# One norm in three FFN stages: a sum over partitions with ones as weights, and the inverse root by ACT's root, DVE's reciprocal and a Newton step

## The chip, the core and the metric

The kernel runs on one core of one Trainium2 chip. The core has a matrix engine (PE, with its weight loads shown apart as PEld), three engines for elementwise work (DVE, ACT and POOL) and a queue that starts DMA transfers (SP). The metric is the device time of one execution in microseconds; the time of the kernel before is the median of three runs. A profiled execution has a time of its own, and a span from its first to its last instruction, which is a little shorter.

## The reference

A decoder trunk of two layers over 256 tokens with 1024 features, all in float32. Each layer is a feed-forward block (FFN), a mixer, and a second FFN, so there are four FFNs. What matters here is how an FFN begins:

```
def _rmsnorm(x, g):
    y = x * rsqrt(mean(x * x, axis=-1) + 1e-6)
    return y * g

h = h + 0.5 * ((silu(n @ w_gate) * (n @ w_up)) @ w_down),   n = _rmsnorm(h, g)
```

`w_gate` and `w_up` are 1024 x 2816, `w_down` is 2816 x 1024. The norm needs, for each token, the sum of the squares of its 1024 features, and one over the root of their mean.

## The kernel before, in words

The residual `hT` lies with features on the 128 partitions (8 tiles of 128) and the 256 tokens along the free dimension. A float32 product is made of two rounded parts, so that two PE passes give nearly full precision: `whi` and `wlo` are the high and low part of a weight chunk, and the activations stand as low and high part side by side. One pair of matmuls in `mm2` is L216 (low weights, 256 columns) and L217 (high weights, 512 columns: low and high part of the activations).

An FFN's `gate_up` goes through 11 blocks `b`. Each block takes four PSUM banks (from pools `acc` and `rot` by turns, four banks each), goes over 8 feature tiles in four steps `c` of one weight chunk each, and makes 8 x 4 = 32 pairs. `evacuate` then adds the two halves of each bank (ACT copy L324, DVE add L326), and `epilogue` multiplies by the norm factor and gates: L381, L382 (silu), L383, L384, L386, L387. Then 22 x 8 = 176 pairs of the down projection follow. The FFN is thus 352 + 176 pairs.

The weights flow by `next_chunk`: a DMA on SP brings a chunk, ACT casts it (`whi`, L169), DVE subtracts (`wlo`, L177). At each step the chunk that PE will use three steps later gets its `wlo`, and the casts run one further ahead. ACT and DVE work strictly in the order in which the program issues their instructions, so whatever stands ahead of a cast or subtraction delays it.

The norm is deferred: matmuls use the activations before scaling, and the factor per token, `rb` (with half of it, `rbh`), is applied in `epilogue`. During the end of the stage before, POOL adds the squares into one 128 x 256 tile (`norm_sq`, L278). What follows is placed by `hooks`, functions called at step `c` of block `b`. For FFN 2 to 4:

```
hooks = {1: {0: lambda: norm_sum(s, sets[0]()), 2: mid}}
```

- Block 1, step 0, `norm_sum`: two fp32 matmuls (L284, 128 x 1 each) sum over partitions, with the tokens going to the partitions; they write a bank of the pool that block 0 used, so they wait until DVE has read that bank. DVE adds epsilon (L287), POOL takes the power -1/2 (L250), splits it (L292, L293) and makes two diagonal matrices of it (L297, four instructions).
- Block 1, step 2, `mid`: `norm_row` spreads the factor over all partitions by four 128 x 128 matmuls with ones as weights (L304, L306). ACT copies the result to `rb` (L309), DVE writes `rbh` (L313), and block 0's epilogue follows (`late(0)`).

FFN 1 (other hooks) and the odd mixer use the same `norm_sum` and `norm_row` at other places.

Of the kernel before, what the change touches and what calls it, by code (L numbers as in the profile page):

```python
# [9 lines left out]
F32 = mybir.dt.float32  # L10
F32R = mybir.dt.float32r
I32 = mybir.dt.int32
AF = mybir.ActivationFunctionType
ALU = mybir.AluOpType
AX = mybir.AxisListType

P = 128
T = 256
TB = T // P
D = 1024  # L20
# [17 lines left out]
EPS = 1e-6  # L38
# [37 lines left out]
def trunk_kernel(  # L76
# [21 lines left out]
    nc = tc.nc  # L98
    PSUM = bass.MemoryType.PSUM

    const = ctx.enter_context(tc.tile_pool(name="const", bufs=1))
# [8 lines left out]
    def nm(s):  # L110
        uid[0] += 1
        return f"{s}_{uid[0]}"
# [7 lines left out]
    def small(shape, tag, bufs=2):  # L120
        return spool.tile(shape, F32, tag=tag, name=nm(tag), bufs=bufs)
# [114 lines left out]
    ones_r = const.tile([P, P], F32R, name="ones_r")  # L236
    nc.gpsimd.tensor_copy(ones_r, ones)
    cmean = const.tile([P, 3], F32, name="cmean")
    for i, n in enumerate((D, QL, KVL)):
        nc.gpsimd.memset(cmean[:, i : i + 1], 1.0 / n)  # L240
    mhalf = const.tile([P, 16], F32, name="mhalf")
    nc.gpsimd.memset(mhalf, -0.5)
    warm = const.tile([P, 2], F32, name="warm")
# [2 lines left out]
    def preload(func):  # L246
        nc.scalar.activation(warm[:, 0:1], ones[:, 0:1], func)
# [23 lines left out]
    def norm_sq(s, k, eng=nc.gpsimd):  # L271
        sq = small([P, T], "sq", bufs=3)
        nc.scalar.activation(sq, hT[:, k, :], AF.Square)
        if s.sum is None:
            s.sum = sq
        else:
            t = small([P, T], "sqsum", bufs=3)
            eng.tensor_add(t, s.sum, sq)  # L278
            s.sum = t

    def norm_sum(s, bank):
        s.bank = bank
# [71 lines left out]
    def ffn(s, nxt_args, sets, first=False):  # L354
        with tc.tile_pool(name=nm("ffn"), bufs=2) as fp:
# [47 lines left out]
            if first:  # L403
                hooks = {0: {1: lambda: nc.sync.dma_start(cst_sb, cst), 2: lambda: squares(range(4)),
                             3: lambda: squares(range(4, KD))},
                         1: {2: lambda: norm_sum(s, sets[0]())}, 2: {1: mid, 3: lambda: late(1)}}
            else:
                hooks = {1: {0: lambda: norm_sum(s, sets[0]()), 2: mid}}
            for b in range(NB):
                held[b] = evacuate(gate_up(b, hooks.get(b, {})))  # L410
                if b > (1 if first else 0):
# [649 lines left out]

    const.tile([P, 88], F32, name="align")
    spool.tile([P, 8], F32, tag="align", name="align_small", bufs=1)
    wu = const.tile([P, T], mybir.dt.bfloat16, name="wu")
    nc.vector.memset(wu, 0.0)
# [7 lines left out]
    s = norm_begin("ffn", 0)  # L1075
# [12 lines left out]
    parts = [emit_split() for _ in range(HEAD)]  # L1088
    seen = set()
    for k, c, cs in head:  # L1090
        if k not in seen:
            if k == 0:
                nc.vector.tensor_scalar(s.xh[:, k, :], hT[:, k, :], pcol(s.gname, s.goff), None,
                                        op0=ALU.mult)
# [5 lines left out]
    s = ffn(s, ("mix", 0), (acc_bank, rot_bank), first=True)  # L1100
# [85 lines left out]
```

## Time and profile before

| | |
|---|---|
| three runs | 896.54, 899.02, 899.45 us; median 899.02 |
| profiled execution, its own time | 896.36 us |
| its span | 894.6 us |
| granted TensorE clock | 0.999 |
| DMA | 164.45 MB, mean 184 GB/s |
| start of FFN 2, 3 and 4 on PE | 266.07, 450.43 and 706.34 us |

The starts of FFN 3 and 4 are those of their first pair. In a row of the timeline the columns are start in us, duration in us, engine, line, operation, output <- inputs, form, count and, in brackets, the idle time before it with what ended it. A row of groups has busy time in us and mean duration in ns behind the first bar. A matmul's duration includes its way through the array, so rows of PE overlap; what one costs is read from the distance between starts.

### The profile page before, as it was taken

How to read it: one execution, taken by the hardware profiler on the slowest of the kernel's cores; microseconds unless marked ns; L12 is line 12 of the kernel's file. 1: busy time of each engine (PE TensorE's matmuls, PEld its weight loads, DVE VectorE, ACT ScalarE, POOL GpSimd, SP SyncE). 2: the span in 40 equal slices, each digit the busy share in tenths (PEclk: the TensorE clock that was granted, in tenths of full speed). 3: DMA queues.
4: the chain of work that ended last, by engine and by line, in shares of the span. 5: the costliest groups of instructions: out<-in, count | busy, mean ns of one | idle time of the engine just before them, and what ended most of it. 6: DMA issues, size and time to landing. Idle time of an engine off the chain costs nothing.

```text
span 894.6 us, 13668 instructions
## 1 busy us (share of the span) xinstructions
PE 886.8 (99%) x5206; PEld 783.3 (88%) x5206; DVE 650.0 (73%) x997; ACT 497.8 (56%) x789; POOL 91.5 (10%) x123
## 2 busy tenths in 40 slices
PE   9999999999999999999999999999999999999998
PEld 7888888899898888888888888888888888888887
DVE  6887778658877877775558777756658878777652
ACT  7565554457675555554446555534545666555430
POOL 0200000118433000000130000001120220000000
PEclk9999999999999999999999999999999999999999
DMA  8675556644344655556644555576535456555750
GB/s 321 191 246 189 188 189 231 187 140 136 106 139 144 219 191 187 192 191 223 209 142 147 190 191 189 194 264 190 170 122 163 172 176 212 187 190 191 256 165 24
DMA packets 60257, 164.45 MB, mean 184 GB/s; under 512 B 5408, under 2 KB 7712, under 8 KB 60192
## 3 DMA queue, kind: packets, MB, share of 16 engines
q1 hardware_dynamic: 59904, 163.28, 54.6%
q8 instruction: 41, 0.67, 0.3%
q10 hardware_dynamic: 288, 0.30, 0.1%
q14 instruction: 24, 0.20, 0.1%
HBM read 162.51 MB, written 1.05 MB: 183 GB/s over the span
## 4 chain that ended last, share of the span: by engine, by line
PE 90%; DVE 5%; POOL 1%; issue 1%; ACT 1%; DMA 1%; SPq 0%; DVEq 0%; ACTq 0%; POOLq 0%
PE acc L217 27%; PE rot L217 27%; PE acc L216 14%; PE rot L216 14%; DVE wlo L177 2%; PE rot L210 1%; PE rot L212 1%; PE rot L211 1%; PE acc L211 1%; PE acc L210 1%; PE acc L212 1%; DMA raw<-w_gu 1%; POOL diag L297 0%; DVE sA L623 0%; DVE z L1006 0%
## 5 line engine op out<-in xcount | busy, mean ns | idle before, releaser
L177 DVE TENSOR_TENSOR wlo<-raw,whi 128x1024 fp32r<-128x1024 f32 (+2 forms) x298 | 352.6, 1226 | 72.0 <-ACT whi L169 72.0
L169 ACT CAST whi<-raw 128x1024 fp32r<-128x1024 f32 (+2 forms) x303 | 301.6, 1044 | 99.6 <-PE acc L217 41.3
L217 PE MATMUL acc<-x,whi 128*128 128x512 f32 x768 | 267.8, 391 | 0.0
L217 PE MATMUL rot<-x,whi 128*128 128x512 f32 x704 | 245.6, 392 | 0.0
L216 PE MATMUL acc<-x,wlo 128*128 128x256 f32 x768 | 216.2, 281 | 0.6 <-DVE wlo L182 0.5
L216 PE MATMUL rot<-x,wlo 128*128 128x256 f32 x704 | 197.5, 281 | 0.3 <-DVE wlo L177 0.3
L217 PEld LDWEIGHTS acc<-x,whi 128*128 128x128 f32 x768 | 143.8, 187 | 31.1
L217 PEld LDWEIGHTS rot<-x,whi 128*128 128x128 f32 x704 | 131.7, 187 | 29.0
L216 PEld LDWEIGHTS acc<-x,wlo 128*128 128x128 f32 x768 | 145.2, 189 | 1.5 <-DVE wlo L182 1.1
L216 PEld LDWEIGHTS rot<-x,wlo 128*128 128x128 f32 x704 | 133.1, 189 | 0.6 <-DVE wlo L177 0.6
L217 PE MATMUL rot<-pp,whi 128*128 128x512 f32 x352 | 122.2, 391 | 0.0
L217 PE MATMUL acc<-pp,whi 128*128 128x512 f32 x352 | 122.2, 391 | 0.0
L216 PE MATMUL rot<-pp,wlo 128*128 128x256 f32 x352 | 98.6, 280 | 0.0
L216 PE MATMUL acc<-pp,wlo 128*128 128x256 f32 x352 | 98.6, 280 | 0.0
L217 PEld LDWEIGHTS rot<-pp,whi 128*128 128x128 f32 x352 | 65.8, 187 | 14.4
L217 PEld LDWEIGHTS acc<-pp,whi 128*128 128x128 f32 x352 | 65.8, 187 | 14.4
L216 PEld LDWEIGHTS rot<-pp,wlo 128*128 128x128 f32 x352 | 66.5, 189 | 0.0
L216 PEld LDWEIGHTS acc<-pp,wlo 128*128 128x128 f32 x352 | 66.5, 189 | 0.0
L324 ACT COPY a<-rot 128x256 f32<-128x256 f32 x88 | 29.9, 374 | 50.5 <-PE rot L217 50.5
L382 ACT ACTIVATE gu<-gu 128x512 f32<-128x512 f32 x44 | 27.8, 632 | 52.1 <-DVE gu L381 52.1
L324 ACT COPY a<-acc 128x256 f32<-128x256 f32 x88 | 29.1, 375 | 49.3 <-PE acc L217 49.3
L326 DVE TENSOR_TENSOR gu<-acc,a 128x256 f32<-128x256 f32 x88 | 31.2, 417 | 29.5 <-ACT a L324 29.5
(250 smaller groups left out, 903.6 us busy)
## 6 DMA issues: line engine op xcount, KB each, us to landing
raw<-w_gu SPq DMA_DIRECT2D x172, 512.0 KB, 4.8
raw<-w_down SPq DMA_DIRECT2D x88, 512.0 KB, 4.7
raw<-ew_out SPq DMA_DIRECT2D x8, 512.0 KB, 3.6
raw<-ow_v SPq DMA_DIRECT2D x8, 512.0 KB, 3.5
raw<-ow_u SPq DMA_DIRECT2D x8, 512.0 KB, 4.9
raw<-ow_out SPq DMA_DIRECT2D x8, 512.0 KB, 3.8
raw<-ew_p SPq DMA_DIRECT2D x4, 512.0 KB, 3.8
raw<-w_gu SPq DMA_DIRECT2D x7, 256.0 KB, 5.3
```

Source lines behind the costliest of these rows:

```text
L169: nc.scalar.copy(hi[:, :n], r[:, :n])
L177: eng.tensor_sub(lo[:, :n], r[:, :n], hi[:, :n].bitcast(F32))
L210: nc.tensor.matmul(out, wl, xh, start=start, stop=False, skip_group_check=True)
L211: nc.tensor.matmul(out, wh, xl, start=False, stop=False, skip_group_check=True)
L212: nc.tensor.matmul(out, wh, xh, start=False, stop=stop, skip_group_check=True)
L216: nc.tensor.matmul(bank[:, 0:T], wl, x[:, 1, :], start=start, stop=False, skip_group_check=True)
L217: nc.tensor.matmul(bank, wh, x.rearrange("p s t -> p (s t)"), start=False, stop=stop, skip_group_check=True)
L324: nc.scalar.copy(tmp[:, i, :], bank[:, 0:T])
L326: nc.vector.tensor_add(out[:, i, :], bank[:, T:], tmp[:, i, :])
L382: nc.scalar.activation(t, t, AF.Silu)
```

## The change

FFN 2 to 4 compute the factor in another way; FFN 1 and the mixers keep theirs.

- `norm_parts`, block 0, step 0: POOL rounds the sum of squares to a high part and subtracts for the low part (two instructions of 128 x 256).
- `norm_all`, block 1, step 0: four 128 x 128 matmuls with ones as weights (L293 of the changed file) sum over partitions and leave the sum in every partition. ACT takes the root of 128 x 256 (with a table load ahead of it) and loads the table of silu again (`preload`). DVE writes the mean plus epsilon.
- `norm_inverse`, block 1, step 1: DVE takes the reciprocal of the root, makes one Newton step (three instructions) and halves the result into `rbh`.
- Block 1, step 2 keeps `late(0)` alone. `norm_sum` and `norm_row` go from these three FFNs.
- A column with epsilon joins the constants, and a filler tile shrinks by as much as that column takes.

```diff
+    eps_col = const.tile([P, 1], F32, name="eps_col")
+    nc.gpsimd.memset(eps_col, EPS)
...
+    def norm_parts(s, fp):
+        s.parts = fp.tile([P, 2, T], F32R, tag="parts", name=nm("parts"), bufs=1)
+        nc.gpsimd.tensor_copy(s.parts[:, 1, :], s.sum)
+        nc.gpsimd.tensor_sub(s.parts[:, 0, :], s.sum, s.parts[:, 1, :].bitcast(F32))
+
+    def norm_all(s, bank, fp):
+
+        for tb in range(TB):
+            ts = slice(tb * P, (tb + 1) * P)
+            for i in range(2):
+                nc.tensor.matmul(bank[:, ts], ones_r, s.parts[:, i, ts], start=tb == 0 and i == 0,
+                                 stop=i == 1, skip_group_check=True)
+        s.root = fp.tile([P, T], F32, tag="root", name=nm("root"), bufs=1)
+        nc.scalar.activation(s.root, bank[:, 0:T], AF.Sqrt, scale=1.0 / D, bias=eps_col)
+        preload(AF.Silu)
+        s.mean = fp.tile([P, T], F32, tag="mean", name=nm("mean"), bufs=1)
+        nc.vector.tensor_scalar(s.mean, bank[:, 0:T], 1.0 / D, EPS, op0=ALU.mult, op1=ALU.add)
+
+    def norm_inverse(s, fp):
+
+        y, t = [fp.tile([P, T], F32, tag=n, name=nm(n), bufs=1) for n in ("inv", "newton")]
+        nc.vector.reciprocal(y, s.root)
+        nc.vector.tensor_mul(t, y, y)
+        nc.vector.scalar_tensor_tensor(t, t, -0.5, s.mean, op0=ALU.mult, op1=ALU.mult)
+        s.rb = small([P, T], "rb", bufs=2)
+        nc.vector.scalar_tensor_tensor(s.rb, t, 1.5, y, op0=ALU.add, op1=ALU.mult)
+        s.rbh = small([P, T], "rbh", bufs=2)
+        nc.vector.tensor_scalar(s.rbh, s.rb, 0.5, None, op0=ALU.mult)
...
-                hooks = {1: {0: lambda: norm_sum(s, sets[0]()), 2: mid}}
+                hooks = {0: {0: lambda: norm_parts(s, fp)},
+                         1: {0: lambda: norm_all(s, sets[0](), fp), 1: lambda: norm_inverse(s, fp),
+                             2: lambda: late(0)}}
...
-    const.tile([P, 88], F32, name="align")
+    const.tile([P, 80], F32, name="align")
```

Where the instructions stand is shown at three places in FFN 2. On PE, at the turn from block 0 (bank pool `rot`) to block 1 (`acc`), before:

```order
L216 MATMUL rot_3056<-x_2455,wlo_2936 128x256
L217 MATMUL rot_3056<-x_2455,whi_2935 128x512
L284 MATMUL rot_3159<-cmean,sqsum_3046 128x1 [waits DVE_49,Pool_49]
L284 MATMUL rot_3159<-cmean,sqsum_3046 128x1
L216 MATMUL acc_3155<-x_2455,wlo_3058 128x256
L217 MATMUL acc_3155<-x_2455,whi_3057 128x512
```

At the same place, in the changed kernel:

```order
L216 MATMUL rot_3058<-x_2457,wlo_2938 128x256
L217 MATMUL rot_3058<-x_2457,whi_2937 128x512
L293 MATMUL rot_3164<-parts_3059,ones_r 128x128 [waits DVE_49,Pool_49]
L293 MATMUL rot_3164<-parts_3059,ones_r 128x128 x3
L216 MATMUL acc_3160<-x_2457,wlo_3063 128x256
L217 MATMUL acc_3160<-x_2457,whi_3062 128x512
```

The two fp32 matmuls have given way to four of 128 x 128, with waits on the same two engines; the four matmuls L304 and L306, which stood 16 pairs later, have no successor.

On ACT, from block 0's last copy to the epilogue of block 0, before:

```order
L324 COPY a_3146<-rot_3056 128x256 [waits PE_49]
L169 CAST whi_3175<-raw_3061 128x1024 [waits DMAHW4_49]
L169 CAST whi_3197<-raw_3083 128x1024 [waits DMAHW5_49,DVE_49]
L309 COPY rb_3223<-rot_3159 128x256 [waits DVE_49,PE_49]
L382 ACTIVATE gu_3145<-gu_3145 128x512 [waits DVE_49]
L386 CAST pp_3052<-gu_3145 128x2x256 [waits DVE_49]
```

The same stretch of ACT in the changed kernel:

```order
L355 COPY a_3151<-rot_3058 128x256 [waits PE_49]
L296 ACT_TABLE_LOAD
L296 ACTIVATE root_3169<-rot_3164,eps_col 128x256 [waits PE_49]
L249 ACT_TABLE_LOAD
L249 ACTIVATE warm<-ones 128x1
L169 CAST whi_3174<-raw_3066 128x1024 [waits DMAHW4_49]
L169 CAST whi_3205<-raw_3088 128x1024 [waits DMAHW5_49,DVE_49]
L413 ACTIVATE gu_3150<-gu_3150 128x512 [waits DVE_49]
L417 CAST pp_3054<-gu_3150 128x2x256 [waits DVE_49]
```

The two casts now stand behind the root and two table loads, and the copy `rb` behind them is gone.

On DVE, from block 0's last addition to the epilogue of block 0, before:

```order
L326 TENSOR_TENSOR gu_3145<-rot_3056,a_3146 128x256 [waits Activation_49]
L287 TENSOR_SCALAR me_3162<-rot_3159 128x2 [waits PE_49]
L177 TENSOR_TENSOR wlo_3124<-raw_2939,whi_3123 128x1024 [waits DMAHW3_49]
L177 TENSOR_TENSOR wlo_3176<-raw_3061,whi_3175 128x1024 [waits DMAHW4_49,Activation_49]
L313 TENSOR_SCALAR rbh_3225<-rot_3159 128x256 [waits Activation_49]
L381 TENSOR_TENSOR gu_3145<-gu_3145,rb_3223 128x512 [waits DVE_49]
```

The same stretch of DVE in the changed kernel:

```order
L357 TENSOR_TENSOR gu_3150<-rot_3058,a_3151 128x256 [waits Activation_49]
L299 TENSOR_SCALAR mean_3172<-rot_3164 128x256 [waits Activation_49]
L177 TENSOR_TENSOR wlo_3129<-raw_2941,whi_3128 128x1024 [waits DMAHW3_49]
L304 RECIPROCAL inv_3196<-root_3169 128x256
L305 TENSOR_TENSOR newton_3197<-inv_3196 128x256 [waits DVE_49]
L306 SCALAR_TENSOR_TENSOR newton_3197<-newton_3197,mean_3172 128x256 [waits DVE_49]
L308 SCALAR_TENSOR_TENSOR rb_3201<-newton_3197,inv_3196 128x256 [waits DVE_49]
L310 TENSOR_SCALAR rbh_3203<-rb_3201 128x256 [waits DVE_49]
L177 TENSOR_TENSOR wlo_3175<-raw_3066,whi_3174 128x1024 [waits DMAHW4_49,Activation_49]
L412 TENSOR_TENSOR gu_3150<-gu_3150,rb_3201 128x512
```

The first instruction behind the additions now waits for ACT, and five instructions stand ahead of the second `wlo`.

## The prediction

> **What bounds the kernel now.** The profile's page comes first: its span, its busy times, and the chain that ended last by engine.
>
> ```profile
> span 894.6 us, 13668 instructions
> PE 886.8 (99%) x5206; PEld 783.3 (88%) x5206; DVE 650.0 (73%) x997; ACT 497.8 (56%) x789; POOL 91.5 (10%) x123
> PE 90%; DVE 5%; POOL 1%; issue 1%; ACT 1%; DMA 1%; SPq 0%; DVEq 0%; ACTq 0%; POOLq 0%
> ```
>
> PE holds 90% of the chain. So the change is worth the PE time that it frees, less any time that it makes PE wait. PE's timeline next, around the two places in FFN 2 where the norm sits (L284 and L304 to L306).
>
> ```profile
> 277.03 0.28 PE L216 MATMUL rot<-x,wlo 128*128 128x256 f32 x1
> 277.50 0.58 PE L284 MATMUL rot<-cmean,sqsum 128*128 128x1 f32 x4
> 278.38 0.28 PE L216 MATMUL acc<-x,wlo 128*128 128x256 f32 x1
> ...
> 283.23 0.28 PE L216 MATMUL acc<-x,wlo 128*128 128x256 f32 x1
> 283.58 0.22 PE L304 MATMUL rot<-diag,ones_r 128*128 128x128 f32 x1
> 284.37 0.28 PE L216 MATMUL acc<-x,wlo 128*128 128x256 f32 x1
> ```
>
> From 278.38 to 283.23 there are 14 pairs, 0.346 us each. In both disturbed stretches two pairs are made as well, so what exceeds 2 x 0.35 is the norm's: 1.35 - 0.70 = 0.65 us for L284, and 1.14 - 0.69 = 0.45 us for the four L304 and L306. The same rows in FFN 3, FFN 4 and, for L284 alone, FFN 1:
>
> ```profile
> 461.18 0.28 PE L216 MATMUL acc<-x,wlo 128*128 128x256 f32 x1
> 461.66 0.58 PE L284 MATMUL acc<-cmean,sqsum 128*128 128x1 f32 x4
> 462.54 0.28 PE L216 MATMUL rot<-x,wlo 128*128 128x256 f32 x1
> 467.39 0.28 PE L216 MATMUL rot<-x,wlo 128*128 128x256 f32 x1
> 468.53 0.28 PE L216 MATMUL rot<-x,wlo 128*128 128x256 f32 x1
> 717.30 0.28 PE L216 MATMUL rot<-x,wlo 128*128 128x256 f32 x1
> 717.77 0.58 PE L284 MATMUL rot<-cmean,sqsum 128*128 128x1 f32 x4
> 718.65 0.28 PE L216 MATMUL acc<-x,wlo 128*128 128x256 f32 x1
> 723.50 0.28 PE L216 MATMUL acc<-x,wlo 128*128 128x256 f32 x1
> 724.64 0.28 PE L216 MATMUL acc<-x,wlo 128*128 128x256 f32 x1
> ...
> 22.73 0.28 PE L216 MATMUL rot<-x,wlo 128*128 128x256 f32 x1
> 23.08 0.50 PE L284 MATMUL acc<-cmean,sqsum 128*128 128x1 f32 x4
> 23.88 0.28 PE L216 MATMUL rot<-x,wlo 128*128 128x256 f32 x1
> ```
>
> FFN 3 gives 1.36 - 0.69 = 0.67 and 1.14 - 0.69 = 0.45 us, FFN 4 1.35 - 0.70 = 0.65 and 0.45 us. All the norm's PE time that the change touches is therefore 1.97 + 1.35 = 3.32 us of the span; no more than that can be freed on PE. In FFN 1 L284 follows one pair (0.35) after 22.73 and costs 1.15 - 0.69 = 0.46 us; in FFN 2 to 4 it starts some 0.13 us after its turn and costs 0.2 more. The reason stands in DVE's timeline in FFN 2 (the fourth row is PE's):
>
> ```profile
> 276.93 1.48 DVE L326 TENSOR_TENSOR gu<-rot,a 128x256 f32<-128x256 f32 x4 [1.95 <-ACT a L324]
> 284.57 0.43 DVE L313 TENSOR_SCALAR rbh<-rot 128x256 f32<-128x256 f32 x1 [3.83 <-ACT rb L309]
> 295.27 4.63 DVE L177 TENSOR_TENSOR wlo<-raw,whi 128x1024 fp32r<-128x1024 f32 x4
> ...
> 297.90 0.28 PE L216 MATMUL rot<-x,wlo 128*128 128x256 f32 x1
> ```
>
> The first of four additions ends near 276.93 + 0.42 = 277.35 us, past the slot for L284 at 277.03 + 0.35 = 277.38 once the signal has travelled; the norm's bank is the one that it reads.
>
> **PE's part of the change.** The fp32 sums and the spreading go, -3.32 us. Four 128 x 128 matmuls with ones as weights come, in the first place's position. They are of the form of L304 and L306, so 0.45 us each time. They write the same pool's bank, so they wait for the same addition: between 0 and 0.2 us more (FFN 1 against FFN 2 to 4). I take the 0.13 by which L284 starts late, since weights that are ones can be loaded during it. That makes 0.58 us three times, 1.74 us, with ends of 1.35 and 1.95. **PE gains 3.32 - 1.74 = 1.6 us, between 1.4 and 2.0.**
>
> **POOL.** Its first instructions must end before block 1. The sum of squares ends here:
>
> ```profile
> 265.62 6.01 POOL L278 TENSOR_TENSOR sqsum<-sqsum,sq 128x256 f32<-128x256 f32 x6
> ```
>
> At 271.63, that is; two more of that size take about 2 us (6.01 / 6 each) and end near 273.6, 3.9 us ahead of the matmuls. The power, the split and the diagonals that POOL loses were waited for by nothing that bounds: PE took up L304 one pair after 283.23. Cost nothing.
>
> **ACT.** Its timeline, in FFN 2 and, for a table load, in FFN 4:
>
> ```profile
> 277.85 2.00 ACT L169 CAST whi<-raw 128x1024 fp32r<-128x1024 f32 x2
> 284.17 0.37 ACT L309 COPY rb<-rot 128x256 f32<-128x256 f32 x1 [4.32 <-PE rot L306]
> 724.83 1.28 ACT L382 ACT_TABLE_LOAD   x1
> 726.13 0.63 ACT L382 ACTIVATE gu<-gu 128x512 f32<-128x512 f32 x1
> ```
>
> After the copies, at 277.85, come a load (to 279.1), the root (0.37 for the copy's size, at most 0.63, the activation of twice the size: to 279.6), the second load (to 280.9), a small activation (0.2, my estimate, below the copy's 0.37) and the two casts, 281.1 to 283.1, which now end 3.3 us later than at 279.85. The 4.32 us in which ACT waited for the spread sum take that up. Six loads come, and the one in FFN 4 goes.
>
> **DVE.** The rows that price its instructions are groups:
>
> ```profile
> L177 DVE TENSOR_TENSOR wlo<-raw,whi 128x1024 fp32r<-128x1024 f32 x292 | 346.3, 1230 | 66.3 <-ACT whi L169 66.3
> L872 DVE RECIPROCAL rs<-sums 128x2 f32<-128x2 f32 x8 | 1.2, 153 | 0.0
> L287 DVE TENSOR_SCALAR me<-acc 128x2 f32<-128x2 f32 x4 | 0.6, 156 | 7.9 <-PE acc L284 7.9
> L1006 DVE SCALAR_TENSOR_TENSOR z<-rot,par_h,row_sb 128x256 f32<-128x256 f32 x6 | 2.6, 478 | 0.0
> ```
>
> `mean` waits for the root, as `rbh` waited for `rb` (both read one bank), so DVE idles from 278.4 to 279.65, and the `wlo` behind it waits too. Then `mean` (0.43, to 280.1), `wlo` (to 281.3), the reciprocal, the product (0.43), two steps of 0.48, the halving (0.43), and the second `wlo`. No row shows a reciprocal of 256 columns. At two columns it takes 153 ns against 156 for a plain instruction, so 0.43 us is the near end, and I take it; from the far side, `wlo` has at most 1.2 ns per column and pass (1230 / 1024), and I carry the case of several passes as a rival. By the near end the chain ends at 283.5 and the second `wlo` at 284.7, and block 0's epilogue starts at 284.7, where it started near 284.9 before.
>
> PE needs the first of these chunks at block 1's fourth step, about 286, and the second at block 2's first, about 289; both are met. The tightest place is later: the first `wlo` of the group at 295.27 ends by 296.5, and PE needs it at block 2's fourth step, 297.90, so 1.4 us are left. After the change PE comes 0.5 us earlier and DVE 0.2, so about **1.1 us of cover are left. The ACT and DVE chain costs nothing, and each us beyond this cover costs one in each of three FFNs.** FFN 3 and 4 have the same order of work.
>
> A rule speaks against this edit: the Trainium skill, in "ScalarE: Activation LUTs", What ACT_TABLE_LOAD costs, counts 1.28 us for a load and 1.38 for a drain at every switch, and advises batching by table set. The trace agrees with the load, 1.28 us, and shows no drain, for the next activation starts 1.30 after it. By the page's sum the chain would be 1.4 us longer on DVE, and the forecast 3 x 0.3 = 0.9 us less of a gain.
>
> **The sum.** 896.36 - 1.6 = 894.8 us for an execution like the profiled one. That one lies 2.66 us under the median of 899.02 (its own time is 1.8 above its span), so against the median: **897.4 us**, 0.18% less. About 0.3%, 2.7 us, is what a measurement of this kernel can tell from no change, so this counts as the same.
>
> **The rivals.** *PE keeps a slower beat* (slower). Its pairs have two paces. In the table by stretch, FFN 2's block 0 before L284 (the columns are length, busy time and count of L217 alone on PE and PEld, clock, DMA):
>
> ```profile
> 266.07:277.03 10.96, 10.84 (x31) 5.83 (x31) 1.00 0.43 139
> ...
> 692.22 0.50 PE L217 MATMUL rot<-zz,whi 128*128 128x512 f32 x1 [0.20 <-DVE zz L1016]
> ```
>
> 31 pairs in 10.96 us are 0.3535 each, at a granted clock of 1.00; after L284 it is 0.346. The second row is a wait after which the same slow pace set in and held until FFN 4's L284. If the new matmuls don't end it as L284 did, the 528 - 32 = 496 later pairs of an FFN cost 496 x 0.007 = 3.5 us. Since a slow FFN 2 hands its pace on to FFN 3, and FFN 4 meets the same, all three is the likelier form: 897.4 + 10.5 = 907.9; FFN 4 alone gives 900.9. Against it: after each group of four short matmuls L304 and L306 the pairs ran at 0.346 to 0.35. But those came out of the quick pace, and the new ones meet the slow one in FFN 2 and 4, with a wait. It makes the kernel slower by over 0.3% from two FFNs on (897.4 + 7.0 = 904.4).
>
> *The reciprocal passes many times over its data.* At eight passes, 8 x 256 x 1.2 ns = 2.5 us, 2.1 more than taken; PE waits 2.1 - 1.1 = 1.0 us in each FFN, 3.0 in all, 897.4 + 3.0 = 900.4, still within 0.3%. For it speaks only that no row is long enough; against it the 153 ns. The Trainium skill, "VectorE: DVE Perf Modes", First, the fixed hardware budget, has the reciprocal as an iterated division with a repeat count of 8. The trace has two columns only, too few to show this.
>
> *The matmuls save nothing*, if bank wait and weights cost what the second place gave up: 899.0. Against it, PE loses a whole place.
>
> *More than 0.3% faster* would take 0.9 of the 1.1 us in each FFN, which four matmuls of 0.45 leave no room for. Only a displacement of the whole measurement, whose runs spread over 2.9 us, could show it.
>
> **How the numbers follow.** Forecast 0.60, the slower beat in two or three FFNs 0.12 and in one 0.03, many passes 0.08, no saving 0.07, faster by more 0.10. Same is 0.60 + 0.03 + 0.08 + 0.07 = 0.78, slower 0.12, faster 0.10. The range goes from the lowest run less the gain, 896.54 - 1.6 = 894.9, to the slower beat in one FFN, 900.9; it takes in the many passes and no saving, and leaves out the slower beat in more FFNs.
>
> **What would show it.** Right: PE's rows have one disturbed stretch per FFN with 1.2 to 1.35 us for two pairs, 0.346 per pair behind it, no PE row with a wait on DVE's `wlo` L177 in blocks 1 and 2, table loads of 1.28 us, and a reciprocal of about 0.43. Wrong: pairs at 0.3535 after block 0, a wait at block 2's fourth step, or the first new matmul more than 0.2 us after its turn.

## The result, and the profile after

The changed kernel takes 902.52 us (median of 9 runs, 899.28 to 905.65); the kernel before, run beside it, 898.74 (9 runs, 895.72 to 900.28). The ratio is 1.0058, with an interval of 1.0041 to 1.0075: slower by 0.6%, where a gain of 0.18% was forecast. The profiled execution took 902.24 us, its span 5.6 us more than the one before. The nine runs lie in three groups some 3 us apart (one at 899.3, four at 902.1 to 902.5, four at 905.1 to 905.7), about what one FFN costs more at the slower of the prediction's two paces, 3.5 us. So the number of FFNs at that pace seems to differ from run to run; in both profiled executions FFN 1 goes at the quicker one. First the changed kernel's page (span, busy times, chain by engine), to be held against the three rows that open the prediction.

```profile
span 900.2 us, 13647 instructions
PE 892.0 (99%) x5194; PEld 782.5 (87%) x5194; DVE 661.7 (74%) x1009; ACT 505.5 (56%) x797; POOL 86.1 (10%) x109
PE 88%; DVE 7%; issue 2%; ACT 1%; POOL 1%; DMA 1%; SPq 0%; DVEq 0%; ACTq 0%; POOLq 0%
```

PE has 12 matmuls fewer and is busy 5.2 us longer. Where that lies is shown by counts in equal stretches. In the table by stretch, for L217 alone as in the prediction, these are 100 us each of FFN 1, FFN 2, FFN 3 and FFN 4:

```profile
80.00:180.00 100.00, 100.00 (x290) 53.94 (x289) 1.00 0.60 202
330.00:430.00 100.00, 100.00 (x285) 53.19 (x284) 1.00 0.60 203
520.00:620.00 100.00, 100.00 (x284) 53.18 (x284) 1.00 0.60 201
770.00:870.00 100.00, 100.00 (x289) 53.87 (x289) 1.00 0.60 200
```

The kernel before has 289 or 290 in all four; its rows of FFN 2 and 3:

```profile
330.00:430.00 100.00, 100.00 (x289) 53.88 (x289) 1.00 0.62 207
520.00:620.00 100.00, 100.00 (x290) 53.89 (x289) 1.00 0.61 199
```

In FFN 2 and 3 the changed kernel makes 4 to 6 fewer at the same granted clock of 1.00: it goes at the slower of the two paces that the prediction described. From the starts to the nanosecond these are 346.7 and 353.3 ns per pair; 6.67 ns apart, 3.5 us for an FFN's 528 pairs.

PE's timeline shows where it starts in FFN 2. The first three rows are at the norm (L293), the last three at block 2's fourth step.

```profile
277.24 0.28 PE L216 MATMUL rot<-x,wlo 128*128 128x256 f32 x1
277.71 0.63 PE L293 MATMUL rot<-parts,ones_r 128*128 128x128 f32 x4
278.59 0.28 PE L216 MATMUL acc<-x,wlo 128*128 128x256 f32 x1
...
297.32 0.28 PE L216 MATMUL rot<-x,wlo 128*128 128x256 f32 x1
297.66 0.32 PE L216 MATMUL rot<-x,wlo 128*128 128x256 f32 x1
298.04 0.28 PE L216 MATMUL rot<-x,wlo 128*128 128x256 f32 x1
```

FFN 2 begins slow in both kernels, and behind the norm the pairs take 346.7 ns here too. The pair begun at 297.66 takes 0.38 us, 0.035 too long, and from there on every pair takes 353.3 ns: the last 440 of FFN 2 and all of FFN 3. What came late is `wlo`; DVE's timeline tells why:

```profile
277.14 1.48 DVE L357 TENSOR_TENSOR gu<-rot,a 128x256 f32<-128x256 f32 x4 [1.18 <-ACT a L355]
279.99 0.43 DVE L299 TENSOR_SCALAR mean<-rot 128x256 f32<-128x256 f32 x1 [1.36 <-ACT root L296]
281.46 1.75 DVE L304 RECIPROCAL inv<-root 128x256 f32<-128x256 f32 x1
...
285.96 0.68 DVE L412 TENSOR_TENSOR gu<-gu,rb 128x512 f32<-128x512 f32 x1
...
296.32 3.49 DVE L177 TENSOR_TENSOR wlo<-raw,whi 128x1024 fp32r<-128x1024 f32 x3
```

The reciprocal takes 1.75 us. Block 0's epilogue starts at 285.96 instead of some 284.9, and the `wlo` group behind it at 296.32 instead of 295.27: 1.05 us later, while PE is there 0.24 us earlier. Of the cover of 1.4 us that the prediction measured, 1.29 is spent on this, and the 0.1 left is less than the weight load ahead of the matmul takes (189 ns, the mean of L216's loads). ACT went as foretold:

```profile
278.18 1.28 ACT L296 ACT_TABLE_LOAD   x1
279.48 0.47 ACT L296 ACTIVATE root<-rot,eps_col 128x256 f32<-128x256 f32 x1
279.97 1.28 ACT L249 ACT_TABLE_LOAD   x1
```

In FFN 3 the norm meets the slow pace, and the pace goes on behind it. In FFN 4 the norm waits; the rows are of PE, of DVE and of POOL:

```profile
464.11 0.28 PE L216 MATMUL acc<-x,wlo 128*128 128x256 f32 x1
464.65 0.63 PE L293 MATMUL acc<-parts,ones_r 128*128 128x128 f32 x4
465.53 0.28 PE L216 MATMUL rot<-x,wlo 128*128 128x256 f32 x1
...
722.54 0.27 PE L216 MATMUL rot<-x,wlo 128*128 128x256 f32 x1
723.86 0.63 PE L293 MATMUL rot<-parts,ones_r 128*128 128x128 f32 x4 [0.81 <-DVE gu L357]
724.74 0.28 PE L216 MATMUL acc<-x,wlo 128*128 128x256 f32 x1
...
717.71 5.68 DVE L177 TENSOR_TENSOR wlo<-raw,whi 128x1024 fp32r<-128x1024 f32 x4 [0.99 <-ACT whi L169]
723.31 1.40 DVE L357 TENSOR_TENSOR gu<-rot,a 128x256 f32<-128x256 f32 x4
...
718.21 1.27 POOL L285 CAST parts<-sqsum 128x256 fp32r<-128x256 f32 x1
719.56 1.60 POOL L286 TENSOR_TENSOR parts<-sqsum,parts 128x256 fp32r<-128x256 f32 x1
```

The same place in the kernel before, on DVE:

```profile
712.08 4.92 DVE L177 TENSOR_TENSOR wlo<-raw,whi 128x1024 fp32r<-128x1024 f32 x4 [0.98 <-ACT whi L169]
```

With POOL's two new instructions beside them the four `wlo` take 5.68 us, not 4.92. The additions that free the norm's bank start only at 723.31, 0.4 after PE's turn, and PE waits 0.81 us.

The time adds up by stage, from start to start on PE. FFN 2 goes from 184.36 to 186.86 us: 440 x 6.67 ns = 2.93 for the pace, 0.04 for the wait, less 0.45 that the norm got shorter (0.65 + 0.45 before, 1.35 - 0.70 = 0.65 after), makes 2.52; measured 2.50. FFN 3 with the stage behind it, up to the wait near that stage's end (the prediction's row at 692.22 us): 528 x 6.67 ns = 3.52, less 0.40 (1.12 to 1.42 - 0.70 = 0.72), makes 3.12; measured 3.08. FFN 4's norm costs 2.20 - 0.70 = 1.50 instead of 1.10, and its first 30 pairs are quick where they were slow; measured 0.17 more. The rest is -0.1: FFN 2 starts 0.22 later, and from that wait to FFN 4 it is 0.34 less, in the main since the pairs there are slow before and quick now.

### The profile page after: what moved, and what is told of

The parts are those of the page before. It is cut to its first block, busy times and chain, and to the rows that moved or that the text cites. A ratio compares the mean times of both kernels' runs of the same rounds, so it can differ in the third digit from the quotient of the medians.

```text
span 900.2 us, 13647 instructions
## 1 busy us (share of the span) xinstructions
PE 892.0 (99%) x5194; PEld 782.5 (87%) x5194; DVE 661.7 (74%) x1009; ACT 505.5 (56%) x797; POOL 86.1 (10%) x109
## 3 DMA queue, kind: packets, MB, share of 16 engines
HBM read 162.51 MB, written 1.05 MB: 182 GB/s over the span
## 4 chain that ended last, share of the span: by engine, by line
PE 88%; DVE 7%; issue 2%; ACT 1%; POOL 1%; DMA 1%; SPq 0%; DVEq 0%; ACTq 0%; POOLq 0%
PE acc L217 26%; PE rot L217 26%; PE acc L216 14%; PE rot L216 13%; DVE wlo L177 2%; PE rot L210 1%; PE rot L212 1%; PE rot L211 1%; DVE par_h L361 1%; PE acc L211 1%; PE acc L210 1%; PE acc L212 1%; DMA raw<-w_gu 1%; ACT whi L169 1%; POOL diag L328 0%
## 5 line engine op out<-in xcount | busy, mean ns | idle before, releaser
L217 PE MATMUL acc<-x,whi 128*128 128x512 f32 x768 | 270.1, 395 | 0.0
L217 PE MATMUL rot<-x,whi 128*128 128x512 f32 x704 | 247.3, 395 | 0.0
L216 PE MATMUL acc<-x,wlo 128*128 128x256 f32 x768 | 216.5, 282 | 0.2
L216 PE MATMUL rot<-x,wlo 128*128 128x256 f32 x704 | 197.6, 281 | 0.3 <-DVE wlo L177 0.3
L217 PEld LDWEIGHTS acc<-x,whi 128*128 128x128 f32 x768 | 144.2, 188 | 33.1
L217 PEld LDWEIGHTS rot<-x,whi 128*128 128x128 f32 x704 | 132.0, 187 | 30.7
L216 PEld LDWEIGHTS acc<-x,wlo 128*128 128x128 f32 x768 | 145.3, 189 | 1.6 <-DVE wlo L182 1.2
L216 PEld LDWEIGHTS rot<-x,wlo 128*128 128x128 f32 x704 | 133.0, 189 | 0.7 <-DVE wlo L177 0.6
L217 PE MATMUL rot<-pp,whi 128*128 128x512 f32 x352 | 123.4, 395 | 0.0
L217 PE MATMUL acc<-pp,whi 128*128 128x512 f32 x352 | 123.4, 395 | 0.0
L216 PE MATMUL acc<-pp,wlo 128*128 128x256 f32 x352 | 98.7, 280 | 0.0
L216 PE MATMUL rot<-pp,wlo 128*128 128x256 f32 x352 | 98.7, 280 | 0.0
L217 PEld LDWEIGHTS rot<-pp,whi 128*128 128x128 f32 x352 | 66.0, 187 | 15.5
L217 PEld LDWEIGHTS acc<-pp,whi 128*128 128x128 f32 x352 | 66.0, 187 | 15.5
L216 PEld LDWEIGHTS rot<-pp,wlo 128*128 128x128 f32 x352 | 66.5, 189 | 0.0
L216 PEld LDWEIGHTS acc<-pp,wlo 128*128 128x128 f32 x352 | 66.5, 189 | 0.0
L357 DVE TENSOR_TENSOR gu<-rot,a 128x256 f32<-128x256 f32 x88 | 31.4, 418 | 29.3 <-ACT a L355 29.3
```

The source lines that it names most:

```text
L216: nc.tensor.matmul(bank[:, 0:T], wl, x[:, 1, :], start=start, stop=False, skip_group_check=True)
L217: nc.tensor.matmul(bank, wh, x.rearrange("p s t -> p (s t)"), start=False, stop=stop, skip_group_check=True)
L357: nc.vector.tensor_add(out[:, i, :], bank[:, T:], tmp[:, i, :])
```

## The experiments

The letters of the theories are those of the text on record ahead of each run, and a letter of one group of runs need not mean the same in the next. Ratios are against runs of the kernel before on the same chip. "Slow" and "quick" mean the pace, 353.3 and 346.7 ns a pair.

**What starts the slow pace?** The kernel before, with a reciprocal that nothing reads behind `late(0)`:

```diff
+            def extra():
+                y = fp.tile([P, T], F32, tag="extra", name=nm("extra"), bufs=1)
+                nc.vector.reciprocal(y, s.rb)
...
-                hooks = {1: {0: lambda: norm_sum(s, sets[0]()), 2: mid}}
+                hooks = {1: {0: lambda: norm_sum(s, sets[0]()), 2: lambda: (mid(), extra())}}
```

> The kernel before with one more DVE instruction, a reciprocal of 128 x 256 into a tile that nobody reads, behind block 0's epilogue in FFN 2 to 4. It takes 1.75 us, the cover at block 2's fourth step was 1.4 us, so the wlo there comes about 0.3 us late. Norm, matmuls, POOL and tables are as before. Theory A: PE waits 0.3 us there in each FFN (0.9), and the beat behind it is 0.3533 in some of the three FFNs until the next norm's fp32 sums end it, 3.1 us for each FFN: 897.3 with none, 900.4 with one, 906.6 with three. Theory B: the beat stays 0.3467 behind that wait, 897.3.

902.26 us, ratio 1.0053 (1.0034 to 1.0072). PE's timeline in FFN 2, block 2's fourth step, and the table by stretch:

```profile
297.54 0.28 PE L216 MATMUL rot<-x,wlo 128*128 128x256 f32 x1
298.12 0.39 PE L216 MATMUL rot<-x,wlo 128*128 128x256 f32 x1
298.58 0.28 PE L216 MATMUL rot<-x,wlo 128*128 128x256 f32 x1
```

```profile
330.00:430.00 100.00, 100.00 (x284) 53.18 (x283) 1.00 0.60 201
520.00:620.00 100.00, 100.00 (x284) 53.18 (x283) 1.00 0.59 200
770.00:870.00 100.00, 100.00 (x290) 53.99 (x289) 1.00 0.59 201
```

Two pairs take 0.58 and 0.46 us, 0.35 over their time; behind them FFN 2 is slow, FFN 3 likewise, FFN 4 waits and stays quick. A late `wlo` alone starts the slow pace, though not every time: in FFN 1, where all kernels wait for a `wlo` at some 49 us, 7 of 20 profiles are slow behind it. The same with two plain products (0.43 us each) in the reciprocal's place:

> As the run with the reciprocal, but with two products of 128 x 256 instead, 0.85 us, which lies within the cover of 1.4 us. Theory A: no wait at block 2's fourth step, 0.3467 behind it, time as before, 896.4 in an execution like the profiled one. A delay that counts whether or not it is covered would give 3 x 0.85 = 2.6 us more, 899.

896.93 us, ratio 0.9996 (0.9984 to 1.0008). As long as DVE stays inside its cover, its extra work costs nothing.

**Is the late `wlo` all?** The changed kernel with `mean` moved from `norm_all` into `norm_inverse`, ahead of the reciprocal and behind the first `wlo`, so that DVE idles 0.23 us for the root and not 1.36:

```diff
-        nc.vector.tensor_scalar(s.mean, bank[:, 0:T], 1.0 / D, EPS, op0=ALU.mult, op1=ALU.add)
+        s.bank = bank
...
+        nc.vector.tensor_scalar(s.mean, s.bank[:, 0:T], 1.0 / D, EPS, op0=ALU.mult, op1=ALU.add)
```

> The changed kernel with one DVE instruction moved: mean stands behind the first wlo of block 1 instead of ahead of it, so that DVE works on that wlo while it would wait for the root; the chain behind ends about 1.2 us earlier. Theory A (late weights set the beat): the wlo for block 2's fourth step, which came 0.04 us late in FFN 2 of the changed kernel, is in time; FFN 2 keeps 0.3467 us per pair behind its norm, FFN 3 takes that over, and the two stages lose the 6.2 us of the slow beat: 896 to 897 us. Theory B (the four matmuls at the norm set the beat, whatever DVE does): 0.3533 in FFN 3 as before, and in FFN 2 from the norm or later: 899 to 902. Theory C (the loss is the sum of waits, the beat is nothing to do with it): 0.1 us less than the changed kernel, 902.

905.74 us, ratio 1.0095 (1.0072 to 1.0119). No `wlo` is late in FFN 2 to 4, and yet FFN 2 and 3 are slow from end to end. The rows of both:

```profile
330.00:430.00 100.00, 100.00 (x284) 53.18 (x284) 1.00 0.58 195
520.00:620.00 100.00, 100.00 (x284) 53.18 (x283) 1.00 0.59 201
```

FFN 2 begins slow, as it does in every profile; behind the norm it is still slow, and FFN 3 is handed the same. So the new matmuls don't end the slow pace every time. Over all profiles with them the pairs went quick behind 7 of the 12 that met it; behind the old sums in the same place of FFN 2 to 4, which waited too, in 7 of 8. These are too few to tell the two apart, but the old kernel had `norm_row` behind them and the new one has nothing. The changed kernel with the old sums (two fp32 matmuls, 128 x 1) put back at block 3, as a reset:

```diff
+            def reset(bank):
+                for tb in range(TB):
+                    nc.tensor.matmul(bank[:, tb : tb + 1], s.sum[:, tb * P : (tb + 1) * P],
+                                     cmean[:, 0:1], start=True, stop=True)
...
+                         3: {0: lambda: reset(sets[0]())}}
```

> The changed kernel with two fp32 matmuls of the old norm (128 x 1, result unused) at block 3's first step in FFN 2 to 4. They cost PE about 0.65 us each time, 2.0 in all. Theories A and B: they end a slow beat as they did in the kernel before; behind block 3 all three FFNs run at 0.3467, so FFN 2 and FFN 3 win back about 2.9 us each of 3.1 and 3.5: 902.2 - 5.8 + 2.0 = 898.4. Theory C: only the cost shows, 904.2. If the slow beat goes on behind them, what ended it in the kernel before was not these matmuls.

905.77 us, ratio 1.0085 (1.0065 to 1.0104). Neither expected time came out. The sums wait for their bank; behind them FFN 2 stays slow, FFN 3 goes from slow to quick, FFN 4 from quick to slow. A group that waits is no sure reset.

**POOL beside DVE.** The changed kernel with one fp32 product of 128 x 256 on the sum itself, without POOL's parts:

```diff
-                nc.tensor.matmul(bank[:, ts], ones_r, s.parts[:, i, ts], start=tb == 0 and i == 0,
-                                 stop=i == 1, skip_group_check=True)
+        nc.tensor.matmul(bank[:, 0:T], ones, s.sum, start=True, stop=True)
...
-                hooks = {0: {0: lambda: norm_parts(s, fp)},
```

> The changed kernel with the sum over partitions as one fp32 128x256 product on the sum of squares itself, in place of GpSimd's two parts and the four 128x128 products. Theory C (FFN4's wait of 0.81 us ahead of the norm comes from the parts on GpSimd running beside VectorE's wlo and slowing both): without the parts the four wlo of FFN4 take 4.9 us as before the change, not 5.7, the additions come earlier, and the wait falls to 0.1 to 0.3; the fp32 product itself takes 0.4 to 0.7 us in place of four times 0.11. With the beat left to chance the time is 899 to 903. Rival (the wait is from the bank's own late addition whatever GpSimd does): the wait in FFN4 stays at 0.6 to 0.9.

904.95 us, ratio 1.0087 (1.0071 to 1.0104). FFN 4 on PE and DVE:

```profile
723.47 0.28 PE L216 MATMUL rot<-x,wlo 128*128 128x256 f32 x1
723.94 0.67 PE L290 MATMUL rot<-sqsum,ones 128*128 128x256 f32 x2
724.80 0.28 PE L216 MATMUL acc<-x,wlo 128*128 128x256 f32 x1
...
718.29 4.93 DVE L177 TENSOR_TENSOR wlo<-raw,whi 128x1024 fp32r<-128x1024 f32 x4 [0.97 <-ACT whi L169]
```

Theory C holds: `wlo` takes 4.93 us again, and the norm costs 1.33 - 0.70 = 0.63, not 1.50. The time rises all the same: FFN 2 and 3 are slow and FFN 4 is from its block 2's fourth step on, where a `wlo` is late. With the stretch ahead of FFN 4 that makes 1559 slow pairs in the profile against 995 of the changed kernel.

**A group that waits for nothing.** In the kernel before, `norm_row`'s four matmuls (L304, L306) had nothing to wait for. e1 with four such products in their old place (`four`: ones by `parts`, into the other half of the norm's bank; nothing reads them):

```diff
-                              2: lambda: late(0)}}
+                              2: lambda: (four(s.bank, s.parts), late(0))}}
```

> The kernel of e1_mean_behind_wlo with, in FFN 2 to 4, four more 128x128 products (ones by the parts of the sums, into the other half of the norm's bank) in block 1 ahead of its third step, where norm_row's four stood before; nothing reads them and they wait for nothing that is still under way. Theory A (the time lost in the changed kernel is TensorE's slower beat, and what used to end it was norm_row's short group that waits for nothing): from that place FFN 2, 3 and 4 show pairs of 346 to 347 ns whatever they had ahead of it, unless a late wlo comes behind it; the four cost 3 x 0.45 us, and the time falls from 905.7 of e1 to 898 to 900, with FFN1's own beat as before. Rival (the group ends nothing; chance or the wait decides): slow pairs go on behind block 1's third step in two of the three FFNs and the time stays at 902 to 907.

897.63 us (897.12 to 900.33, 12 runs), ratio 1.0008 (0.9996 to 1.0020): 8 us less than e1, with 12 matmuls more, and a little under the expected range. The profiled run doesn't show the group at work, since behind its norms the pace was quick already; that the group did it is concluded from the 12 runs, against e1's 902.35 to 908.96. The changed kernel with the same group at block 3, behind the late `wlo`:

```diff
+                         3: {2: lambda: four(sets[0](), s.parts)}}
```

> The changed kernel with, in FFN 2 to 4, the same four 128x128 products that nothing reads, ahead of block 3's third step, into a bank that is free by then: behind the late wlo of block 2 instead of ahead of it. Theory A (a short group without a wait ends the slower beat): FFN 2, 3 and 4 show 346 to 347 ns a pair from block 3's third step on; a slow stretch lasts at most from block 2's fourth step to there (some 60 pairs, 0.4 us each FFN); the four cost 3 x 0.45; the time falls from 902.5 to 897.5 to 899.5. Rival (only the place at block 1 or the wait decides): slow pairs go on behind block 3 where they went on in the changed kernel, and the time is 903 to 904.

900.98 us, ratio 1.0036 (1.0021 to 1.0050), above the expected range, and 898.22 in the profiled run. There FFN 2 and 3 go from slow to quick at the group: 78 pairs of 353.3 ns ahead of it, more than 400 of 346.7 behind it. So far theory A stood. Then a kernel that needs no wait at all: the fp32 product at block 0's fourth step, into a free bank, with root and reciprocal right behind it:

```diff
+                hooks = {0: {3: lambda: (norm_all(s, sets[1](), fp), norm_inverse(s, fp))},
+                         1: {2: lambda: late(0)}}
```

> The sum over partitions as one fp32 128x256 product, a block's step earlier, in a bank of the other set that is free, with root, mean, reciprocal and Newton step right behind it and the late epilogue at block 1's third step as before the change. No bank is waited for, and VectorE has the reciprocal done before the late epilogue and its wlo. Theory A (a late wlo and a waiting norm start the slower beat): nothing starts it in FFN 2 to 4, no wlo is late at block 2's fourth step, and the norm costs TensorE 0.5 to 0.7 us an FFN where the four products with their wait cost 0.65 to 1.5: 895 to 897.5, with FFN1's beat as before. Rival (a norm without norm_row's group keeps whatever beat it meets, and FFN 2 to 4 meet a slow one): 899 to 906.

904.13 us, ratio 1.0079 (1.0061 to 1.0097). Nothing waits, but FFN 2 to 4 start slow and stay slow to the end. To it were added one, then four products of ones by ones at block 1's first step (`short`), then four in FFN 1 as well (block 4's third step), and four in FFN 1 of the kernel before alone; the one version writes `range(1)`:

```diff
+            def short(bank):
+                for i in range(4):
+                    o = T + i % TB * P
+                    nc.tensor.matmul(bank[:, o : o + P], ones_r, ones_r, start=i == 0, stop=True,
+                                     skip_group_check=True)
...
+                         1: {0: lambda: short(s.bank), 2: lambda: late(0)}}
...
+                         4: {2: lambda: short(sets[1]())}}
```

> The kernel of e6_norm_a_step_earlier with, in FFN 2 to 4, one 128x128 product (ones by ones, into the other half of the norm's bank, waited for by nothing and read by nothing) ahead of block 1's first step. Theory A1 (any short product that waits for nothing ends the slower beat): pairs of 346 to 347 ns behind it in FFN 2, 3 and 4; the time falls from 904.1 to 894.5 to 895.5 (three times 0.11 for the product, three times 3.3 saved). Theory A4 (it takes the group of four): the slow pairs go on, 904 to 905. Rival B (what ended the beat in the runs before was not the group): slow pairs go on here and in the next kernel too.

> The same with four such products at the same place. Theory A: pairs of 346 to 347 ns behind them in FFN 2, 3 and 4; 895 to 896, or 3 us above it in the runs in which FFN1 goes slow. Rival B: the slow pairs go on and the time is 904 to 906.

> The same as the one before, with four such products in FFN1 too, ahead of block 4's third step, behind the stretch of FFN1 (46 to 52 us) where its wlo comes late. Theory A: no FFN goes slow behind its group; all runs lie within 1 us, at 895.5 to 896.5, under all runs of the kernel before. Rival B: two groups of runs 3 us apart are left.

> The kernel before with the four products in FFN1 alone, at the same place. Theory A (the kernel's own runs at 899 are those in which FFN1 keeps the slower beat): the runs at 899 are gone, all lie at 896.3 to 897.6, 0.45 us above the kernel's own lower group. Rival B: both groups stay, 896 and 899.

907.59, 907.73, 909.50 and 899.36 us; ratios 1.0099 (1.0081 to 1.0117), 1.0086 (1.0059 to 1.0114), 1.0104 (1.0079 to 1.0129) and 0.9997 (0.9985 to 1.0009). In none of their profiles did an added product end the slow pace, and e12 kept runs at 899 to 900 (7 of 12). In e7's FFN 3 it went the other way: behind the norm's fp32 product the pairs were quick, and eight pairs later the one added product, which waited for nothing, made them slow again. Theory A fell: a group without a wait is not enough.

**Which pair it falls behind.** In the slow pace the gap from L217's start to the next one isn't even: it runs 232, 241, 236 ns in turn over three pairs. These are the gaps ahead of a product that waits for nothing, the gap that the turn would bring next (the gap due, within 1 ns), and the pace behind it, from the starts to the nanosecond:

```
kernel, start (us)     gaps ahead (ns)       due   pair behind (ns)
e6  275.19             241 236 232 241       236   353.3   fp32 product
e9  281.02             233 241 236 233       241   353.3   four of 128 x 128
e12  58.41             232 241 235 232       241   353.3   four of 128 x 128
e8  306.63             236 233 241 236       232   346.7   four of 128 x 128
```

Over all profiles up to e12, without exception: where such a product met the slow pace, the pace behind the fp32 product was slow where 236 was due and quick once, where 232 was due; behind the added four of 128 x 128 it was slow where 241 was due and quick where 232 was. (`norm_row`'s own four are not among these: behind them the pace was quick, whatever was due.) This is theory D: the place in the turn decides. It says what eight pairs more (two thirds of a turn, e13) and 24 pairs more (eight whole turns, e14) must do. The last line is FFN 1's, 8 pairs later: e15 is the kernel before with it, e16 is e13 with it.

```diff
-                         1: {0: lambda: short(s.bank), 2: lambda: late(0)}}
+                         1: {1: lambda: short(sets[0]()), 2: lambda: late(0)}}
...
+                         1: {2: lambda: late(0), 3: lambda: short(sets[0]())}}
...
+                         4: {3: lambda: short(sets[1]())}}
```

> e9_earlier_and_four_products with the four products one step, 8 pairs, later: ahead of block 1's second step (their result goes into a bank of the other set). In the slower beat the gap from the 512-column matmul to the next runs 232, 241, 236 ns in turn over three pairs. Theory D (how a group that waits for nothing leaves the beat depends on which of the three pairs it falls behind): in e9 and e11 it always fell in the gap of 241 and always left the slow beat, in e8 in that of 232 or 233 and left the fast one; 8 pairs later is two pairs further round, the gap of 232, so FFN 2, 3 and 4 go fast behind it: 895.5 to 897 with FFN1 fast, 898.5 to 900 with FFN1 slow. Rival (what the product's data, weights or place in the kernel are, not the pair): slow as in e9, 902 to 910.

> The same with the four products 24 pairs later than in e9, ahead of block 1's fourth step, into the same other set of banks. Theory D: 24 pairs are eight whole turns, the gap is 241 again, and FFN 2, 3 and 4 stay slow: 904 to 910 as in e9. Rival (the other set of banks, or a later place, makes the difference in the kernel before this): fast, as that one.

> e12_before_and_ffn1 with FFN1's four products 8 pairs later, ahead of block 4's fourth step. Theory D: where FFN1 goes slow at 49 us, the products fall in the gap of 232 and end it; the runs at 899 to 900 are gone and all lie at 896.5 to 898. Rival: two groups of runs, 896.7 and 899.6, as in e12.

> Both together: e13 with FFN1's four products at e15's place. Theory D: no FFN keeps the slow beat behind its group, and all runs lie within 1.5 us at 895.5 to 897. Rival: as e11, 903 to 910.

e14: 903.46 us (902.45 to 906.63), slow in all three FFNs behind the gap of 241, as D has it, though the median lies just under the range. e15: 897.19 us (896.66 to 897.87, 12 runs), ratio 0.9990 (0.9979 to 1.0001), where 7 of the 17 runs of the kernel before lay at 899.32 to 900.33: no run is up there any more, as D has it, though e15's own profile met FFN 1 quick. e16's FFN 1 was slow until the four products (30 pairs of 353.5 ns) and quick behind them (374 of 346.7); its rows by stretch, ahead of them and behind:

```profile
52.90:61.40 8.50, 8.50 (x25) 4.51 (x24) 1.00 0.94 309
61.90:71.90 10.00, 9.82 (x29) 5.44 (x29) 1.00 0.50 179
```

In FFN 2 to 4, however, e13 (905.80 us) and e16 (905.43 us) prove nothing on the four products: their bank wasn't free, and they waited, here in e13:

```profile
281.47 0.66 PE L434 MATMUL rot<-ones_r 128*128 128x128 f32 x4 [0.21 <-DVE gu L354]
```

In e13's FFN 3 the norm's fp32 product, which waited for nothing, fell where 241 was due, and the pairs behind it were quick.

So the last two kernels add no product in FFN 2 to 4 and wait for nothing there. e17 is e6 with the fp32 product one pair later (a hook in `gate_up`, ahead of the second of the step's eight pairs); e18 is e17 with e15's group in FFN 1:

```diff
-                hooks = {0: {3: lambda: (norm_all(s, sets[1](), fp), norm_inverse(s, fp))},
+                hooks = {0: {(3, 1): lambda: (norm_all(s, sets[1](), fp), norm_inverse(s, fp))},
...
+                            if (c, kc * 4 + i) in hooks:
+                                hooks[c, kc * 4 + i]()
```

> e6_norm_a_step_earlier with its fp32 product one pair of matmuls later: behind the first of the eight pairs of block 0's fourth step instead of ahead of it. Nothing else changes and nothing is added. Theory D (where in the slow beat's turn of three pairs a product falls that waits for nothing decides the beat behind it): in e6, e7, e9, e11 and e14 the product fell where the gap of 236 ns was due and left the slow beat, each time; in e7 and e13 it fell once each where 232 and 241 were due and left the fast one. One pair later the gap due is 232: FFN 2, 3 and 4 show 346 to 347 ns a pair behind the product, and the time falls by three times 3.3 us, from 904.1 to 894.5 to 895.5, or 897.5 to 898.5 in the runs in which FFN1 goes slow. Rival (the beat behind the norm is set by something else, such as the waits of other engines or chance): 903 to 908 as e6.

> The same with e15's four products in FFN1 (block 4's fourth step), 0.45 us. Theory D: FFN1 goes fast there in every run, and all runs lie at 895 to 896.2, in one group, below the lower group of the kernel before (896.4 to 897.2). Rival: 903 to 908.

e17: 897.11 us (894.05 to 898.43, 11 runs), ratio 0.9991 (0.9978 to 1.0005), against e6's 904.13 (903.75 to 907.68), 1.0079, on another chip. Its runs lie in two groups, four at 894.1 to 895.1 and seven at 896.9 to 898.4, each reaching some 0.5 us below the expected range. FFN 2 and 4 by stretch (FFN 3 is alike), first e6, then e17:

```profile
330.00:430.00 100.00, 100.00 (x284) 53.18 (x283) 1.00 0.59 201
...
770.00:870.00 100.00, 100.00 (x284) 53.20 (x284) 1.00 0.57 195
```

```profile
330.00:430.00 100.00, 100.00 (x290) 54.02 (x289) 1.00 0.61 207
...
770.00:870.00 100.00, 100.00 (x289) 53.86 (x289) 1.00 0.59 200
```

The one product of each of the three FFNs, moved by one pair, saves 7 us. The product in FFN 2 fell where 232 was due (gaps 236, 232, 240, 236), and the pairs behind it take 346.7 ns; in FFN 4 likewise, and in FFN 3 it met the quick pace. e18: 895.28 us (894.76 to 898.58, 12 runs), ratio 0.9981 (0.9969 to 0.9993). Ten of its runs lie at 894.8 to 895.8, as expected; two at 898.2 and 898.6 are a miss that no profile shows. It is the only version whose interval lies under 1, by 0.2%, and its profiled span is the shortest:

```profile
span 893.1 us, 13634 instructions
```

## Why the prediction was wrong

- **PE keeps a slower beat** was a rival at 0.15, and it is what happened, in two FFNs. Its road, new matmuls that don't end the slow pace, was FFN 3's alone: in FFN 2 they ended it, and the late `wlo` started it again. The rival was held unlikely because "after each group of four short matmuls L304 and L306 the pairs ran at 0.346 to 0.35". That was the evidence for the old place, which the change takes away. `norm_row`'s group ended the slow pace in all 9 cases in which the traces of the runs show it meeting it without a wait; the new group waits for its bank, and behind a wait both paces occur. The rival's price, 7.0 us for two FFNs, was near: 440 + 528 pairs make 6.5.
- **"Each us beyond this cover costs one in each of three FFNs"** is the step that failed most: it priced a wait at its own length. FFN 2 overran its cover by 0.035 us and paid 2.9, since the wait turned the pace, and nothing turned it back until FFN 3 was through; FFN 3 paid 3.5 without a late `wlo` of its own. The rivals of the beat and of the reciprocal were priced as if each stood alone; one set off the other.
- **The reciprocal**, taken at 0.43 us from a row of two columns, takes 1.75. The rival with 2.5 had the better bound: that a short row hides the rate was said, and then the near end was chosen. The groups of the changed kernel, with the mean in ns behind the busy time:

```profile
L304 DVE RECIPROCAL inv<-root 128x256 f32<-128x256 f32 x3 | 5.2, 1746 | 0.0
L299 DVE TENSOR_SCALAR mean<-rot 128x256 f32<-128x256 f32 x2 | 0.9, 426 | 1.9 <-ACT root L296 1.9
```

  From 153 ns at 2 columns to 1746 at 256 it is 6.3 ns a column, against (426 - 156) / 254 = 1.06 for a plain step: six passes. The Trainium skill, "VectorE: DVE Perf Modes", First, the fixed hardware budget, gives the division a repeat count of 8; the trace agrees in kind and shows somewhat less.
- **POOL: "Cost nothing"** failed in FFN 4. Its end was in time, though its two instructions took 1.27 + 1.60 us and not about 2; but beside it DVE's four `wlo` took 0.76 us more, and 0.81 of waiting came of it; e10 shows it. The Trainium skill, "SBUF — State Buffer", SBUF: two separate sides, has a port pair that DVE and POOL share under an exclusive lock. The rows of this case agree: in the kernel before, POOL's addition of 128 x 256 takes 0.74 us where it starts first (706.88 us), and DVE's step L268 beside it 0.83 instead of 0.48; where a `wlo` runs already (270.02) the addition takes 1.60. So POOL's 1.27 + 1.60 seem to hold waiting of its own, and DVE's loss of 0.76 doesn't speak against a full block.
- **PE gains 1.6 us**: the freed 3.32 were right, the new matmuls cost 0.65, 0.72 and 1.50 instead of 0.58 each, so 0.45 was left.
- **ACT** was right. The loads took 1.28 us each and the root 0.47; the root started 1.30 after its load, so the drain that the Trainium skill counts in "ScalarE: Activation LUTs", What ACT_TABLE_LOAD costs, isn't seen here either. DVE's idle time for the root, 1.25 us by the prediction, was 1.36.
- The range's upper end, 900.9, left out the slow beat in two FFNs, though the text itself named the slow beat in all three as the likelier form of the rival. All three of the prediction's signs of being wrong are in the trace: slow pairs, a wait at block 2's fourth step, and in FFN 4 the first new matmul some 1 us after its turn.

Open is why the gap of 232 ends the slow pace, why `norm_row`'s four end it behind 241 too (7 cases) where four products of ones don't (11), and what decides behind a wait.

## What to carry to other kernels

Where one engine's stream sets the time, look at its rate per instruction in equal stretches before counting what an edit saves: here two rates 1.9% apart cost 6.5 us, where the edit freed 0.45. An instruction group that is removed may have been holding the rate; a wait of a few ns may change it for hundreds of instructions, so a cover that is nearly used up is worth more than its length. And an operation that the trace shows only at a tiny size has no price yet: the far bound belongs in the forecast's sum, above all where cover is short.

## What the runs showed of the hardware

The stream of 256- and 512-column matmuls, each with its own weights, has two steady rates at a granted clock of 1.00: 346.7 ns a pair (gaps of 230 and 117) and 353.3 (232, 241, 236 and some 117). It stays at one for hundreds of pairs, until something interrupts it. Where products that waited for nothing interrupted the slow rate, the rate behind each kind of product went by its place in the turn of three pairs, without an exception in these traces. Behind the fp32 product of 128 x 256 it was slow in 18 of 18 cases where 236 was due, quick in all 5 where 232 was and in the one where 241 was; behind FFN 1's two fp32 sums (L284 of the kernel before) it was slow in 6 of 6 where 236 was due and quick in 2 of 2 where 232 was; behind the four of 128 x 128 that the runs added it was slow in 11 of 11 where 241 was due and quick in 3 of 3 where 232 was, but behind `norm_row`'s four it was quick in 7 of 7 where 241 was due and 2 of 2 where 236 was. The fp32 product costs PE 0.42 us with nothing to wait for, no more than four of 128 x 128 on parts that POOL must make first. In e6's timeline two pairs and the product take 1.13 us, less 2 x 0.353:

```profile
274.83 0.28 PE L216 MATMUL rot<-x,wlo 128*128 128x256 f32 x1
275.19 0.59 PE L290 MATMUL acc<-sqsum,ones 128*128 128x256 f32 x2
275.96 0.28 PE L216 MATMUL rot<-x,wlo 128*128 128x256 f32 x1
```
